# Attention of a two-layer decoder trunk: two units under way, scores and maxima of the next unit ahead of the current one's transposes

## The chip, the cores and the metric

The kernel runs on one core of one Trainium2 chip. The metric is device time in microseconds (us). Within the core, TensorE (PE) multiplies matrices into PSUM, VectorE (DVE) does elementwise work and reductions, ScalarE (ACT) does exponentials, copies and casts, GpSimd (POOL) does elementwise work in SBUF, and SyncE (SP) issues DMAs. Each engine works through its own list of instructions in order and waits on the others by semaphores.

## The reference, cut to what matters

A layer of gated DeltaNet comes first and is not touched. The second layer is sparse attention with three branches over 256 tokens. The change lies in its branches, its gate projection and its output projection:

```
q = rope(proj[..., :1024])                 # 16 heads of 64, 4 key groups
z = proj[..., 1024:4096]                   # one gate of 64 for each head and branch
sc = einsum(q, k_cmp) * scale;  p_cmp = masked_softmax(sc, ...);  o_cmp = p_cmp @ v_cmp
ss = einsum(q, ks) * scale;     p_sel = masked_softmax(ss, ...);  o_sel = p_sel @ vs
sw = einsum(q, kw) * scale;     p_win = masked_softmax(sw, ...);  o_win = p_win @ vw
o = sum over branches of sigmoid(gates) * o_branch * silu(z)
y = o @ w_out;  x = layer_norm(alpha * x + y)
```

With 256 tokens all four selection blocks are chosen, so that a query sees 256 keys in the selection branch, 256 in the window branch and 16 compressed ones.

## The kernel before, in words

The 256 tokens are two tiles of 128, t = 0 and t = 1. Attention is cut into 24 **units**: a unit of the first tile holds two heads (their later keys are masked, so that 128 keys each remain), a unit of the second tile holds one head with all 256 keys. The string `UNITS` says in which order the units of the two tiles follow each other. A unit (t, h) goes through these steps, whose names are those of tiles in the traces:

- `scores`: four PE matmuls into `s` (PSUM, two buffers, L1318).
- `maxima`: DVE adds the masks in `s` and reduces the maxima `mx` (L1331 to L1334 for a unit of the second tile, L1327 to L1329 for the first).
- `exps`: ACT's exponentials `pt` and `Pc` (L1351, L1352; L1347, L1348).
- `transposes`: four PE transposes into `ptp` (L1360), and one of `Pc` (L1362) where a pair of heads is complete. `ptp` lies in the PSUM bank `t`, of which there is one.
- `probs`: ACT copies `ptp` to SBUF as `PT` (L1367), and `PcT` (L1371).
- `readout`: PE multiplies with the values into `op` (L1386, L1389, L1392). `op` lies in the PSUM bank `o`, of which there is one. A unit of the second tile writes half of a bank, the odd head of a pair the other half. When the pair is complete `total`, five DVE operations (L1400 to L1404), scales and sums `op` into `zz`; it is deferred and put down at the next `step()`.

Three sorts of work stand among these steps. `fill(n)` takes n pieces from a list and puts them on PE. First these are pieces of the gate projection `pbz` (six matmuls of 512 columns, L233 to L235), then of the output projection: `pbo` for the first tile and `pbl` for the second (twelve of 256 columns). A piece calls for its weight, whose rounding is an ACT cast (`hi_`, L181) and whose remainder is a POOL subtraction (`lo_`, L185). Four pieces end a bank of `pbz`; ACT's `th` and DVE's `zz` (L1218, L1219) follow. `presplit()` puts down one cast ahead. A **merge** (`merge`, L1413) transposes finished columns of the output on PE into `tp_b` (L1418), which is in the same single bank `t` as `ptp`; ACT (`x1h`, L1422) and then DVE (`x1l`, L1423) read it out. Merges make the pieces of the output projection possible.

Nothing reorders these: each engine has them as the loop over the units (L1477 to L1508) writes them down. `FA[i]` and `FB[i]` are the numbers of pieces in the two places of iteration i. Before the change one unit is begun and transposed in the same iteration, and the unit before it is read out between:

```
scores(i)  [maxima(i) for a first-tile unit before the merges]  probs(i-1)  maxima(i)
fill(FA[i])  merge  presplit  exps(i)  readout(i-1)  fill(FB[i])  transposes(i)
```

The last projection pieces come after the loop.

Of the kernel before, what the change touches and what calls it, by code (L numbers as in the profile page):

```python
# [34 lines left out]

FIRST = (1, 2)

UNITS = "001010101101101101111111"
FA = "3113111011210212044211123"
FB = "0211121311122110212111000"  # L40

PRE, TAIL = 4, 2
NEG = -1e30
# [50 lines left out]
def trunk(ctx: ExitStack, tc: tile.TileContext, I: dict, out: bass.AP):  # L94
# [9 lines left out]
    def defer(n, f):  # L104
        late.append([n, f])

    def step():
        for e in late:
            e[0] -= 1
        due = [e for e in late if e[0] <= 0]  # L110
        late[:] = [e for e in late if e[0] > 0]
        for _, f in due:
            f()
# [82 lines left out]
    def lower():  # L196
        while lows:
            lows.pop(0)()
# [42 lines left out]
    def presplit():  # L241
        oldest = next(i for i, n in enumerate(uses) if n)
        split_to(min(state["top"] + PRE, oldest + NSPL, state["s"] + 1))
        lower()

    def fill(n, low=True):
        for _ in range(n):
            step()
            if fills:
                fills.pop(0)()  # L250
            if low:
                lower()
# [25 lines left out]
    first = ring.tile([P, 1024], F32, tag="raw", name="raw_first", bufs=NRAW)  # L278
# [731 lines left out]
    def sbank(name):  # L1010
        return ps_.tile([P, 2, 512], F32, tag="s", name=name)
# [4 lines left out]
    def obank(name):  # L1016
        return pt_.tile([P, 512], F32, tag="o", name=name)
# [203 lines left out]
    def zview(t, c0, n):  # L1221
        i, o = c0 // 1536, c0 % 1536
        return zz[2 * t + i][:, o:o + n]

    def need_z(t, cols):
        while not all((c, t) in zdone for c in range(-(-cols // 512))):
            fill(1)
# [76 lines left out]
    order1 = [(1, h) for h in range(16)]  # L1304
    units = [order0.pop(0) if k == "0" else order1.pop(0) for k in UNITS]
    S_, PT_, PTT, PC, PCT, MX, TP = {}, {}, {}, {}, {}, {}, {}
    cnt = {"n": 0}

    def scores(u):
        t, h = u  # L1310
        sp = S_[u] = sbank(f"s{t}{h}")
        for j in range(2):
            hh = h + j if t == 0 else h
            lq = qT[hh // 8][:, hh % 8, t * P:(t + 1) * P]
            n = 272 if t == 0 or j == 0 else 256
            c0 = 272 if t == 1 and j == 1 else 0
            for i, kk in enumerate((kh, kl)):
                PE.matmul(sp[:, j, 0:n], lq, kk[:, hh // 4, c0:c0 + n], start=i == 0, stop=i == 1)  # L1318

    def maxima(u):  # L1320
        t, h = u
        sp = S_[u]
        cm = cb[:, C_CM0:C_CM0 + 272] if t == 0 else cb[:, C_CM1:C_CM1 + 272]
        mx = MX[u] = sm.tile([P, 6], F32, tag="mx", name=f"mx{t}{h}", bufs=4)
        s4 = sp[:, :, 0:256].rearrange("p j (b k) -> p j b k", b=2)
        if t == 0:
            V.tensor_tensor(sp[:, :, 0:272], sp[:, :, 0:272], cm[:, None, :].to_broadcast([P, 2, 272]), op=ALU.add)  # L1327
            V.tensor_reduce(mx[:, 0:4].rearrange("p (j b) -> p j b", j=2), s4, axis=AX.X, op=ALU.max, negate=True)
            V.tensor_reduce(mx[:, 4:6], sp[:, :, 256:272], axis=AX.X, op=ALU.max, negate=True)  # L1329
        else:  # L1330
            V.tensor_tensor(sp[:, 1, 0:256], sp[:, 1, 0:256], cm[:, 0:256], op=ALU.add)  # L1331
            V.tensor_tensor(sp[:, 0, 256:272], sp[:, 0, 256:272], cm[:, 256:272], op=ALU.add)
            V.tensor_reduce(mx[:, 0:2], s4.rearrange("p j b k -> p b j k"), axis=AX.XY, op=ALU.max, negate=True)
            V.tensor_reduce(mx[:, 4:5], sp[:, 0, 256:272], axis=AX.X, op=ALU.max, negate=True)  # L1334

    def exps(u):
        t, h = u
        sp, mx = S_[u], MX[u]
        s4 = sp[:, :, 0:256].rearrange("p j (b k) -> p j b k", b=2)
        pt = PT_[u] = wk.tile([P, 2, 2, P], F32, tag="hl", name=f"pt{t}{h}", bufs=3)  # L1340
        if t == 0 or h % 2 == 0:
            PC[t, h] = wk.tile([P, 2, 16], F32, tag="Pc", name=f"Pc{t}{h}", bufs=4)
        Pc = PC[t, h - h % 2]
        if t == 0:
            for j in range(2):
                for b in range(2):
                    S.activation(pt[:, j, b, :], s4[:, j, b, :], AF.Exp, bias=mx[:, 2 * j + b:2 * j + b + 1])  # L1347
                S.activation(Pc[:, j, :], sp[:, j, 256:272], AF.Exp, bias=mx[:, 4 + j:5 + j])  # L1348
        else:
            for b in range(2):  # L1350
                S.activation(pt[:, :, b, :], s4[:, :, b, :], AF.Exp, bias=mx[:, b:b + 1])  # L1351
            S.activation(Pc[:, h % 2, :], sp[:, 0, 256:272], AF.Exp, bias=mx[:, 4:5])  # L1352
# [22 lines left out]
    def readout(t, h, half=None):  # L1375

        g_ = h // 4
        if half != 1:
            need_z(t, (h + 2) * 192)
            OP[t] = obank(f"op{t}{h}")  # L1380
        o3 = OP[t][:, 0:390].rearrange("p (r b d) -> p r b d", r=2, b=3)
        for r in range(2) if half is None else (half,):
            PT = PTT[0, h] if t == 0 else PTT[1, h + r]
            for b in range(2):
                if t == 0:
                    PE.matmul(o3[:, r, 1 + b, :], PT[:, r, b, :], vt_[:, b, 0, g_, :], start=True, stop=True)  # L1386
                else:
                    for j in range(2):
                        PE.matmul(o3[:, r, 1 + b, :], PT[:, j, b, :], vt_[:, b, j, g_, :], start=j == 0, stop=j == 1)  # L1389
        if half == 0:  # L1390
            return
        PE.matmul(o3[:, :, 0, :], PCT[t, h], vbd[:, g_, :, :], start=True, stop=True)  # L1392
        rc = sm.tile([P, 2, 3], F32, tag="rc", name=f"rc{t}{h}")
        o4 = o3[:, :, :, 0:64]

        o_ = zview(t, h * 192, 128).rearrange("p (r d) -> p r d", r=2)

        def total():

            V.reciprocal(o3[:, :, :, 64], o3[:, :, :, 64])  # L1400
            V.tensor_tensor(rc, o3[:, :, :, 64], gt[:, t, h * 3:h * 3 + 6].rearrange("p (r b) -> p r b", b=3), op=ALU.mult)
            V.tensor_tensor(o4, o4, zview(t, h * 192, 384).rearrange("p (r b d) -> p r b d", r=2, b=3), op=ALU.mult)
            V.tensor_tensor(o4, o4, rc[:, :, :, None].to_broadcast([P, 2, 3, 64]), op=ALU.mult)
            V.tensor_reduce(o_, o4.rearrange("p r b d -> p r d b"), axis=AX.X, op=ALU.add)  # L1404
            summed.add((t, h))

        defer(1, total)
# [45 lines left out]
    def add_bo(t, pairs):  # L1453
        for c, part in pairs:
            fills.append(lambda c=c, part=part: bo_unit(t, c, part))

    merges, ready = [], []
    cnt["t0"] = 0

    def advance():  # L1460
        if merges:
            merges.pop(0)()

    def merge0(q):
        merge(0, 4 * q, 4, tbank)
        if q:
            add_bo(0, [(c, part) for c in range(2) for part in range(4)])

    def merge1(g_):
        need_z(1, 3072)  # L1470
        merge(1, 2 * g_, 2, tbank)
        add_bo(1, [(0, g_)])
        if g_ == 3:
            add_bo(1, [(1, g_)])

    n = len(units)
    for i in range(n + 1):  # L1477
        if i < n:
            scores(units[i])
        first = i < n and units[i][0] == 0 and not merges  # L1480
        if first:

            maxima(units[i])
        if i:
            probs(units[i - 1])
        step()
        if i < n and not first:
            maxima(units[i])
        fill(int(FA[i]))
        advance()  # L1490
        presplit()
        if i < n:
            exps(units[i])
        if i:
            t, h = units[i - 1]
            if t == 0:
                readout(t, h)
                if h == 14:
                    cnt["t0"] = 1
                    merges += [lambda: merge0(0), lambda: merge0(1)] + ready  # L1500
            else:

                if (units[i - 2] if h % 2 else units[i]) == (1, h ^ 1):
                    readout(t, h - h % 2, h % 2)
                elif h % 2:
                    readout(t, h - 1)
                if h % 4 == 3:
                    (merges if cnt["t0"] else ready).append(lambda g_=h // 4: merge1(g_))  # L1508
        fill(int(FB[i]))
        if i < n:  # L1510
            transposes(units[i])
    while len(merges) > 1:
# [78 lines left out]
```

## Time and profile before

| what | value |
|---|---|
| median of 3 runs | 393.89 us (393.65 to 393.94) |
| the profiled execution: its own time | 393.75 us |
| its span, first to last instruction | 391.9 us |
| PE busy | 379.6 us, 97% of the span |
| DVE, ACT, POOL busy | 223.6, 220.6, 246.3 us |
| mean granted clock of TensorE | 0.994 |

The profiled execution took 393.75 us, of which 391.9 are the span and some 1.85 lie around it. A row of a timeline gives the start in us from the span's beginning, the duration, the engine, the line, the operation with output and input, the number of instructions merged into the row and, in brackets, the idle time ahead of it with what ended it. Matmuls are pipelined: a row's duration is longer than the distance from its start to the next start, so that PE's pace is read from starts.

### The profile page before, as it was taken

The page shows a single profiled execution, that of the slowest core. Times are in us where ns is not written, and L with a number is a line of the kernel's source. Part 1 is how long each engine was busy: PE and PEld are TensorE (multiplying, and loading weights), DVE is VectorE, ACT ScalarE, POOL GpSimd, SP SyncE. Part 2 cuts the span into 40 slices and gives each one's busy share as a digit, 9 for nine tenths or more (in the row PEclk, how much of TensorE's full clock was granted, in tenths as well). Part 3 has the DMA queues.
Part 4 walks back from the last instruction along what each step waited for, and adds up shares of the span by engine and source line. Part 5 has one row for each costly group of instructions (what it writes and reads, how often), then busy time and mean ns, then how long its engine had stood idle before and what let it go on. Part 6 is the DMA issues. An engine that isn't in the chain of part 4 may idle for free.

```text
span 391.9 us, 7551 instructions
## 1 busy us (share of the span) xinstructions
PE 379.6 (97%) x2870; PEld 335.5 (86%) x2870; DVE 223.6 (57%) x591; ACT 220.6 (56%) x433; POOL 246.3 (63%) x154
## 2 busy tenths in 40 slices
PE   8999999999999999999999999999999999999991
PEld 6999999999989987877998788888888888878891
DVE  2868776668623445463641755545656465676726
ACT  4688666656663462625563649566474747456410
POOL 5699999747444846894764988193544637209051
PEclk9999999999999999999999999999999999999997
DMA  7876578654334315573736764243415243301011
GB/s 226 324 223 221 206 232 291 190 135 164 110 110 138 125 35 186 163 248 125 204 118 214 278 223 150 103 153 115 164 39 175 64 153 109 107 3 54 3 54 54
DMA packets 23476, 58.68 MB, mean 150 GB/s; under 512 B 6672, under 2 KB 9232, under 8 KB 23312
## 3 DMA queue, kind: packets, MB, share of 16 engines
q1 hardware_dynamic: 23232, 58.13, 44.9%
q8 instruction: 22, 0.36, 0.4%
q14 instruction: 14, 0.11, 0.1%
q10 hardware_dynamic: 144, 0.07, 0.1%
q0 software_dynamic: 64, 0.01, 0.0%
HBM read 55.96 MB, written 2.23 MB: 148 GB/s over the span
## 4 chain that ended last, share of the span: by engine, by line
PE 42%; DVE 4%; ACT 3%; DMA 2%; POOL 2%; issue 1%; POOLq 0%; DVEq 0%; SPq 0%; ACTq 0%
PE pbz L233 6%; PE pbz L234 6%; PE pbz L235 6%; PE op L1389 4%; PE s L1318 3%; PE ptp L1360 3%; PE op L1392 2%; PE op L1386 1%; DMA raw_bz<-in_bz 1%; ACT hi_bq L181 1%; POOL lo_bq L185 1%; PE pskv L235 1%; PE pbo L233 1%; PE pskv L233 1%; PE pskv L234 1%; PE qtp L1205 1%
## 5 line engine op out<-in xcount | busy, mean ns | idle before, releaser
L185 POOL TENSOR_TENSOR lo_bz<-raw_bz,hi_bz 128x1024 fp32r<-128x1024 f32 x24 | 56.8, 2387 | 39.3 <-ACT hi_bz L181 21.7
L185 POOL TENSOR_TENSOR lo_wqkv<-raw_wqkv,hi_wqkv 128x1024 fp32r<-128x1024 f32 x22 | 52.6, 2408 | 6.7 <-ACT hi_wqkv L181 4.5
L233 PE MATMUL pbz<-hi_bz,x1h 128*128 128x512 f32 x96 | 38.9, 405 | 0.0
L234 PE MATMUL pbz<-hi_bz,x1l 128*128 128x512 f32 x96 | 37.7, 393 | 0.0
L235 PE MATMUL pbz<-lo_bz,x1h 128*128 128x512 f32 x96 | 37.6, 392 | 0.0
L185 POOL TENSOR_TENSOR lo_bo<-raw_bo,hi_bo 128x1024 fp32r<-128x1024 f32 x8 | 18.9, 2390 | 22.8 <-ACT hi_bo L181 17.7
L185 POOL TENSOR_TENSOR lo_skv<-raw_skv,hi_skv 128x1024 fp32r<-128x1024 f32 x12 | 28.4, 2399 | 5.0 <-PE pskv L235 5.0
L185 POOL TENSOR_TENSOR lo_wz<-raw_wz,hi_wz 128x1024 fp32r<-128x1024 f32 x8 | 19.4, 2440 | 16.9 <-ACT hi_wz L181 16.8
L1367 ACT COPY PT<-ptp 128x512 f32<-128x512 f32 x24 | 14.1, 588 | 24.0 <-PE ptp L1360 24.0
L181 ACT CAST hi_bz<-raw_bz 128x1024 fp32r<-128x1024 f32 x24 | 25.2, 1052 | 2.9 <-DMA raw_bz<-in_bz 1.6
L185 POOL TENSOR_TENSOR lo_wo<-raw_wo,hi_wo 128x1024 fp32r<-128x1024 f32 x8 | 18.9, 2385 | 11.5 <-ACT hi_wo L181 11.5
L185 POOL TENSOR_TENSOR lo_bq<-raw_bq,hi_bq 128x1024 fp32r<-128x1024 f32 x8 | 19.1, 2394 | 10.8 <-ACT hi_bq L181 10.8
L181 ACT CAST hi_wqkv<-raw_wqkv 128x1024 fp32r<-128x1024 f32 x22 | 22.7, 1043 | 1.0 <-DMA raw_wqkv<-in_wqkv 1.0
L233 PEld LDWEIGHTS pbz<-hi_bz,x1h 128*128 128x128 f32 x96 | 18.0, 188 | 4.1
L235 PEld LDWEIGHTS pbz<-lo_bz,x1h 128*128 128x128 f32 x96 | 18.0, 188 | 4.1
L234 PEld LDWEIGHTS pbz<-hi_bz,x1l 128*128 128x128 f32 x96 | 18.0, 188 | 2.7
L1351 ACT ACTIVATE pt<-s,mx 128x256 f32<-128x256 f32 x32 | 13.4, 472 | 11.0 <-DVE mx L1334 8.8
L215 PE MATMUL pk<-xh,hi_wqkv 128*128 128x256 f32 x64 | 18.7, 291 | 0.0
L215 PE MATMUL pq<-xh,hi_wqkv 128*128 128x256 f32 x64 | 18.5, 289 | 0.0
L217 PE MATMUL pq<-xh,lo_wqkv 128*128 128x256 f32 x64 | 18.1, 283 | 0.0
L216 PE MATMUL pk<-xl,hi_wqkv 128*128 128x256 f32 x64 | 18.1, 283 | 0.0
L217 PE MATMUL pk<-xh,lo_wqkv 128*128 128x256 f32 x64 | 18.1, 283 | 0.0
(360 smaller groups left out, 1256.1 us busy)
## 6 DMA issues: line engine op xcount, KB each, us to landing
raw_bz<-in_bz SPq DMA_DIRECT2D x24, 512.0 KB, 3.3
raw_wqkv<-in_wqkv SPq DMA_DIRECT2D x23, 512.0 KB, 4.5
raw_skv<-in_skv SPq DMA_DIRECT2D x12, 512.0 KB, 3.3
raw_wz<-in_wz SPq DMA_DIRECT2D x8, 512.0 KB, 3.4
raw_wo<-in_wo SPq DMA_DIRECT2D x8, 512.0 KB, 3.3
raw_bq<-in_bq SPq DMA_DIRECT2D x8, 512.0 KB, 3.7
raw_bo<-in_bo SPq DMA_DIRECT2D x8, 512.0 KB, 3.3
raw_w<-in_w SPq DMA_DIRECT2D x4, 512.0 KB, 3.4
```

Of the source, the lines that this page charges most:

```text
L181: S.copy(h, r)
L185: e.tensor_tensor(l, r, h.bitcast(F32), op=ALU.subtract)
L215: PE.matmul(ps[:, 0:T], wh[:, kt, :], ah[:, kt, :], start=kt == 0, stop=False)
L216: PE.matmul(ps[:, 0:T], wh[:, kt, :], al_[:, kt, :], start=False, stop=False)
L217: PE.matmul(ps[:, 0:T], wl[:, kt, :], ah[:, kt, :], start=False, stop=kt == 7)
L233: PE.matmul(ps, ah[:, kt, tt], wh[:, k4, cols], start=kt == 0, stop=False)
L234: PE.matmul(ps, al_[:, kt, tt], wh[:, k4, cols], start=False, stop=False)
L235: PE.matmul(ps, ah[:, kt, tt], wl[:, k4, cols], start=False, stop=kt == 7)
L1318: PE.matmul(sp[:, j, 0:n], lq, kk[:, hh // 4, c0:c0 + n], start=i == 0, stop=i == 1)
L1351: S.activation(pt[:, :, b, :], s4[:, :, b, :], AF.Exp, bias=mx[:, b:b + 1])
L1367: S.copy(PT.rearrange("p a b c -> p (a b c)"), TP[u])
L1389: PE.matmul(o3[:, r, 1 + b, :], PT[:, j, b, :], vt_[:, b, j, g_, :], start=j == 0, stop=j == 1)
```

## The change

Each iteration now begins the next unit. Its scores and maxima stand behind the readout of the unit before, its exponentials at the end, ahead of the current unit's transposes:

```
probs(i-1)  fill(FA[i])  presplit  readout(i-1)
scores(i+1)  maxima(i+1)  merge  fill(FB[i])  exps(i+1)  transposes(i)
```

The first unit is begun ahead of the loop. `UNITS` puts the eight first-tile units at the places 0, 1, 4, 5, 7, 9, 10 and 11 of 24 (before: 0, 1, 3, 5, 7, 10, 13 and 16). `FA` is 2 up to iteration 13 and 1 from there on; `FB` is 1 up to iteration 12, then 0 1 0 1 0 1 and then 0. Readouts are grouped by the rule of before.

```
-UNITS = "001010101101101101111111"
+UNITS = "001100101000111111111111"
...
     n = len(units)
+
+    def begin(u):
+        scores(u)
+        maxima(u)
+
+    begin(units[0])
+    fill(1)
+    exps(units[0])
     for i in range(n + 1):
-        if i < n:
-            scores(units[i])
-        first = i < n and units[i][0] == 0 and not merges
-        if first:
-
-            maxima(units[i])
         if i:
             probs(units[i - 1])
         step()
-        if i < n and not first:
-            maxima(units[i])
-        fill(int(FA[i]))
-        advance()
+        merge_ = merges.pop(0) if merges else None
+        fill(int(FA[i]) - (i == 0))
         presplit()
-        if i < n:
-            exps(units[i])
         if i:
...
+        if i + 1 < n:
+            begin(units[i + 1])
+        if merge_:
+            merge_()
         fill(int(FB[i]))
+        if i + 1 < n:
+            exps(units[i + 1])
         if i < n:
             transposes(units[i])
```

What this moves is shown at three places. In the names `s114` is the score bank of tile 1, head 14; the other names go the same way, and the number behind the underscore is the tile's own.

First PE, around the merge `tp_b12` of the second tile. Before:

```order
L1318 MATMUL s113_4275<-kl_2283,qT1_2691 128x256
L233 MATMUL pbo00_4198<-hi_bo_3_4005,x1h_2043 128x512
...
L1418 MATMUL tp_b12_4297<-ident_112,zz2_3270 128x128 x2
L1389 MATMUL op112_4306<-vtok_2284,PT112_4280 128x65 x4
L233 MATMUL pbo10_4314<-hi_bo_4_4199,x1h_2043 128x512
...
L1360 MATMUL ptp113_4321<-ident_112,pt113_4302 128x128 x4
```

And in the change:

```order
L1389 MATMUL op18_4187<-vtok_2284,PT18_4175 128x65 x4
L1318 MATMUL s110_4192<-kh_2282,qT1_2691 128x272
L1318 MATMUL s110_4192<-kl_2283,qT1_2691 128x272
L1318 MATMUL s110_4192<-kh_2282,qT1_2691 128x256
L1318 MATMUL s110_4192<-kl_2283,qT1_2691 128x256
L1418 MATMUL tp_b12_4202<-ident_112,zz2_3275 128x128 x2
L1360 MATMUL ptp19_4212<-ident_112,pt19_4166 128x128 x4
L1362 MATMUL s19_4141<-ident_112,Pc18_4111 32x128
```

Before, a readout and a piece of six matmuls stood between the merge's transposes and the next use of the bank `t`; now `ptp19` follows at once.

Second PE at the end of the units. Before:

```order
L1389 MATMUL op114_4405<-vtok_2284,PT114_4377 128x65 x4
L1360 MATMUL ptp115_4410<-ident_112,pt115_4401 128x128 x4
L1362 MATMUL s115_4372<-ident_112,Pc114_4357 32x128
...
L1389 MATMUL op114_4405<-vtok_2284,PT115_4416 128x65 x4
L1392 MATMUL op114_4405<-vbd_2386,PcT114_4418 128x2x65
```

And in the change:

```order
L1318 MATMUL s115_4433<-kl_2283,qT1_2691 128x256
L1360 MATMUL ptp114_4447<-ident_112,pt114_4400 128x128 x4
L1389 MATMUL op114_4459<-vtok_2284,PT114_4452 128x65 x4
L1360 MATMUL ptp115_4464<-ident_112,pt115_4443 128x128 x4
L1362 MATMUL s115_4433<-ident_112,Pc114_4401 32x128
L1389 MATMUL op114_4459<-vtok_2284,PT115_4470 128x65 x4
L1392 MATMUL op114_4459<-vbd_2386,PcT114_4472 128x2x65
```

Before, 36 matmuls of `pbl` stood where the dots are, and 12 of `pbo` between `s115` and `op114`; now no projection stands between `s115` and the end of the readouts.

Third DVE and ACT in the last units. DVE's row around the sum of `op112` in the change (before, the five operations on `op112` stood ahead of the four on `s115`):

```order
L1331 TENSOR_TENSOR s115_4433<-s115_4433,cb_2278 128x256
L1332 TENSOR_TENSOR s115_4433<-s115_4433,cb_2278 128x16
L1333 TENSOR_REDUCE mx115_4438<-s115_4433 128x2
L1334 TENSOR_REDUCE mx115_4438<-s115_4433 128x1
L1400 RECIPROCAL op112_4380<-op112_4380 128x6
L1401 TENSOR_TENSOR rc112_4432<-op112_4380,gt_2972 128x6
L1402 TENSOR_TENSOR op112_4380<-op112_4380,zz3_3805 128x6x64
L1403 TENSOR_TENSOR op112_4380<-op112_4380,rc112_4432 128x6x64
L1404 TENSOR_REDUCE zz3_3805<-op112_4380 128x128
```

And ACT's row around the exponentials of unit 113 in the change:

```order
L1351 ACTIVATE pt113_4348<-s113_4338,mx113_4343 128x2x128 x2
L1352 ACTIVATE Pc112_4292<-s113_4338,mx113_4343 128x16
L1367 COPY PT112_4357<-ptp112_4352 128x512
L945 ACTIVATE x1_2042<-x1_2042,nb_blw0_4312,mv_blw0_4308 128x512
L1422 CAST x1h_2043<-tp_b14_4395 128x2x128
```

The copy `PT` of a unit now stands behind the exponentials of the unit after it (before, it stood ahead of them), and the sum of a finished pair behind the maxima of a unit begun later.

## Rows read from the trace of the kernel before

**Rows 1.** All that PE waited for from 250 us on: total, times, longest.

```profile
PE op L1389 <- DVE zz L1404: 0.6, 2, 0.4
PE tp_b L1418 <- ACT PT L1367: 0.2, 1, 0.2
```

**Rows 2.** PE's timeline through one iteration without a wait.

```profile
351.30 0.60 PE L1360 MATMUL ptp<-ident,pt 128*128 128x128 f32 x4
...
351.76 0.37 PE L1318 MATMUL s<-kh,qT 128*128 128x272 f32 x1
...
352.33 0.39 PE L233 MATMUL pbo<-hi_bo,x1h 128*128 128x512 f32 x1
...
353.72 0.38 PE L1418 MATMUL tp_b<-ident,zz 128*128 128x128 f32 x2
353.94 1.00 PE L1389 MATMUL op<-vtok,PT 128*128 128x65 f32 x8
...
355.29 0.50 PE L233 MATMUL pbo<-hi_bo,x1h 128*128 128x512 f32 x1
...
356.79 0.60 PE L1360 MATMUL ptp<-ident,pt 128*128 128x128 f32 x4
357.14 0.37 PE L1318 MATMUL s<-kh,qT 128*128 128x272 f32 x1
```

**Rows 3.** PE's timeline around the first tile's two merges.

```profile
342.95 0.28 PE L1318 MATMUL s<-kl,qT 128*128 128x256 f32 x1
343.37 0.66 PE L1418 MATMUL tp_b<-ident,zz 128*128 128x128 f32 x4
344.21 2.00 PE L1389 MATMUL op<-vtok,PT 128*128 128x65 f32 x16 [0.19 <-DVE zz L1404]
...
347.42 0.28 PE L1318 MATMUL s<-kl,qT 128*128 128x256 f32 x1
347.89 0.65 PE L1418 MATMUL tp_b<-ident,zz 128*128 128x128 f32 x4 [0.19 <-ACT PT L1367]
348.91 1.11 PE L1389 MATMUL op<-vtok,PT 128*128 128x65 f32 x8 [0.37 <-DVE zz L1404]
```

**Rows 4.** DVE's timeline: maxima, a pair's sum, a merge's remainder, a gate.

```profile
341.34 0.69 DVE L1219 SCALAR_TENSOR_TENSOR zz<-th,pbz 128x512 f32<-128x512 f32 x1 [0.49 <-ACT th L1218]
...
345.36 0.17 DVE L1334 TENSOR_REDUCE mx<-s 128x1 f32<-128x16 f32 x1
345.44 0.68 DVE L1423 TENSOR_TENSOR x1l<-tp_b,x1h 128x512 fp32r<-128x512 f32 x1
...
352.54 0.43 DVE L1331 TENSOR_TENSOR s<-s,cb 128x256 f32<-128x256 f32 x1 [1.71 <-PE s L1318]
...
353.83 0.16 DVE L1334 TENSOR_REDUCE mx<-s 128x1 f32<-128x16 f32 x1
354.55 0.43 DVE L1423 TENSOR_TENSOR x1l<-tp_b,x1h 128x256 fp32r<-128x256 f32 x1 [0.55 <-ACT x1h L1422]
...
365.67 0.20 DVE L1400 RECIPROCAL op<-op 128x6 f32<-128x6 f32 x1 [0.42 <-PE op L1392]
...
367.31 0.56 DVE L1404 TENSOR_REDUCE zz<-op 128x128 f32<-128x384 f32 x1
```

**Rows 5.** ACT's timeline: exponentials and copies of second-tile units.

```profile
345.62 0.84 ACT L1351 ACTIVATE pt<-s,mx 128x256 f32<-128x256 f32 x2 [0.97 <-DVE mx L1334]
...
347.25 0.59 ACT L1367 COPY PT<-ptp 128x512 f32<-128x512 f32 x1 [0.63 <-PE ptp L1360]
...
350.32 0.84 ACT L1351 ACTIVATE pt<-s,mx 128x256 f32<-128x256 f32 x2 [1.15 <-DVE mx L1334]
...
351.20 1.05 ACT L181 CAST hi_bo<-raw_bo 128x1024 fp32r<-128x1024 f32 x1
```

**Rows 6.** Stretches at the end: length, busy of PE, PEld, DVE, ACT, POOL; PEclk, DMA.

```profile
384.00:385.00 1.00, 0.05 (x1) 0.00 (x0) 0.97 (x3) 0.00 (x0) 0.00 (x0) 1.00 0.00 0
...
386.00:387.00 1.00, 0.00 (x0) 0.00 (x0) 0.91 (x2) 0.00 (x0) 0.92 (x2) 0.94 0.00 0
```

More of the change, by code (lines that the diff above doesn't have):

```diff
@@ L36 @@
 FIRST = (1, 2)
-UNITS = "001010101101101101111111"
-FA = "3113111011210212044211123"
-FB = "0211121311122110212111000"
+UNITS = "001100101000111111111111"
+FA = "2222222222222211111111111"
+FB = "1111111111111010101000000"
 PRE, TAIL = 4, 2
@@ L1497, in trunk @@
                 readout(t, h)
[L1498 to L1508, printed above, removed]
+            elif (units[i - 2] if h % 2 else units[i] if i < n else 0) == (1, h ^ 1):
+                readout(t, h - h % 2, h % 2)
+            elif h % 2:
+                readout(t, h - 1)
+            if (t, h) == (0, 14):
+                cnt["t0"] = 1
+                merges += [lambda: merge0(0), lambda: merge0(1)] + ready
+            if t and h % 4 == 3:
+                (merges if cnt["t0"] else ready).append(lambda g_=h // 4: merge1(g_))
+        if i + 1 < n:
+            begin(units[i + 1])
+        if merge_:
+            merge_()
         fill(int(FB[i]))
+        if i + 1 < n:
+            exps(units[i + 1])
         if i < n:
```

## The prediction, as it was made

> **What bounds the kernel now.** I read the waits first. From the start of the attention on, PE waited three times, 0.8 us in all [rows 1]. PE's timeline shows the same: one block starts where the last leaves off, with a piece of projection between any two steps of a unit [rows 2]. So PE's list of work is the bound, and the change leaves that list as it is in content: the same matmuls in another order. The time can only move by what PE waits, and by what a change of operand type costs. Around the first tile's merges PE loses more than the page's waits say [rows 3]: 0.42 and 0.47 us from the last score matmul to the merge, where the spacing of 0.23 us for 512 columns (1.39 us for six, [rows 2]) gives 0.12 for 256, and 0.84 and 1.02 us for four merge transposes, where two take 0.22 [rows 2]. That is 0.30 + 0.35 + 0.40 + 0.58 = 1.63 us. The readouts behind those waits last 0.11 us more than plain ones (1.11 against 1.00, [rows 2, 3]), twice: 1.85 us. This is all that a better order could take away.
>
> **PE's cover.** I price each block by its distance to the next [rows 2]: a piece behind scores 1.39 us, a piece behind float32 work (transposes, a readout) 1.50, `ptp` 0.35, with `Pc` 0.46, a merge of two transposes 0.22, of four 0.44. A piece of `pbl`, twelve matmuls of half the columns, is taken as a piece of six, 1.50.
>
> **The chains that must fit under it.** Let T be the end of the scores that an iteration begins. DVE starts on them 0.21 us later (352.33 to 352.54, [rows 2, 4]). The four operations run 1.29 us to the start of the last, and DVE can start something else 0.08 behind that (345.36 to 345.44): T + 1.58. The maxima themselves are there 0.09 later, T + 1.67. ACT starts the exponentials 0.09 after the maxima (345.53 to 345.62, [rows 4, 5]) and is free 0.88 later (350.32 to 351.20). Three things now stand behind these on their engines:
> - ACT's copy `PT` of the unit before: 1.67 + 0.09 + 0.88 + 0.59 + 0.05 until PE goes on (347.84 to 347.89, [rows 3, 5]) = **T + 3.27**. The next readout waits for it.
> - DVE's sum of a finished pair: 2.20 us (365.67 to 367.87, [rows 4]); 1.58 + 2.20 + 0.05 = **T + 3.83**. The next readout that opens the bank `o` waits for it; the bank is single, and the row of before shows exactly this wait [rows 1].
> - DVE's `x1l` of a merge, 0.43 us, or 0.68 for a merge of four: **T + 2.06 or T + 2.31**. The next `ptp` waits for it, since `ptp` and `tp_b` share the bank `t`. The trace of before has no such wait, because a readout and a piece stand between; its bounds are nothing and these two numbers, and I take these, since the order of the change puts `x1l` behind the four operations on the scores and `ptp` directly behind `tp_b`.
>
> **Iterations 0 to 12.** Behind the scores stand a piece, `ptp` and two pieces: 1.39 + 0.35 + 1.50 + 1.39 = 4.63 us. The longest chain is the sum with a gate's `zz` ahead of it (0.62 us from start to start of a following operation, taken as 0.69 less the 0.08 overlap): 4.45 us. It is covered, by 0.2 us; the copy by 1.3 us. So no gain there, since there was no wait before [rows 1], and no loss.
>
> **Iterations 13 to 23,** with one piece ahead of the readout and mostly none behind the scores. PE's waits, one after the other:
> - 13: merge of four, then `ptp` at once: 2.31 - 0.44 = 1.87.
> - 14: merge of four and a piece, 1.94, `ptp` waits 0.37 and goes on at 2.31; behind 0.35 + 1.50 the readout would start at 4.16, but DVE has maxima, `x1l`, a gate and a sum, 1.58 + 0.60 + 0.62 + 2.20 + 0.05 = 5.05: 0.89 more. 1.26.
> - 15, 17, 21: merge of two, then `ptp`: 2.06 - 0.22 = 1.84 each, 5.52. The piece behind `ptp` then covers the copy.
> - 16, 18: a piece, `ptp`, a piece, 3.24, against the sum's 3.83: 0.59 each, 1.18.
> - 19: `ptp` with `Pc` and a piece, 1.96, against the copy's 3.27: 1.31.
> - 20: `ptp` and a piece, 1.85, against the sum's 3.83: 1.98.
> - 22: `ptp` alone, 0.35, against the sum's 3.83: 3.48.
> - 23: the last `ptp` runs 0.60 us, then 0.59 for the copy and some 0.1 for two handovers, 1.29 - 0.46 = 0.83 before the last readout.
>
> Together 17.43 us. Each iteration then lasts 5 to 6.5 us, longer than DVE's 1.58 + 0.43 + 2.20 in it, so that DVE is free at each T, as assumed. Of the twelve waits seven are ahead of a readout, which then lasts 0.11 more: 0.8. Those ahead of `ptp` I cost at nothing more (bound 0.1 each).
>
> **Changes of type.** The first piece behind float32 work costs 1.50 - 1.39 = 0.11 us more than one behind scores [rows 2]. Such a change from float32 to the rounded type occurs 39 times in the attention before and 46 times in the change's order, because scores stand alone between a readout and `ptp` in the late iterations: 7 x 0.11 = 0.8 us.
>
> **What moves for nothing.** The maxima a unit ahead and the exponentials ahead of `ptp` take `ptp`'s own wait away; there was hardly one to take. The first-tile units moved up bring the merges five iterations earlier; the output projection then runs between the last units, where it covers, and is missing behind them: the 36 matmuls of `pbl` ahead of the last readout are gone from there, which is what 22 and 23 pay. From the last readout on, PE's list is the same in both, and so is the layer norm's tail. Casts and remainders are as many as before and are called for a unit earlier or later; their cover is the weights that are kept ahead, and if it were gone a piece would wait for at most a cast and a remainder.
>
> **The sum:** 393.75 + 17.43 + 0.8 + 0.8 - 1.85 = 410.9 us, 4.3% above. The profiled execution is 0.14 us under the median of the runs, so I say **411.0**.
>
> **The rivals.**
> - *TensorE's clock falls in the longest wait.* At the end of the trace the last matmul ends at 384.05, the granted clock is full from 384 to 385, and its mean is 0.94 from 386 to 387 [rows 6]: with nothing to do it went to the lower level, half, within 3 us. The wait of iteration 22, 3.5 us, is as long. What follows on PE is some 10 us of matmuls; at half speed to the end that is up to 10 us more, for a part of them 2 to 3 us: 413 to 414, at most 421. Against it: the readout and `ptp` stand on either side, and no wait inside the trace of before was long enough to show it. The Trainium skill's page "TensorE: Matmul & The Clock Gate", section "Why this matters for your kernels", warns of this: idle gaps between bursts of matmuls take the clock to its lower level, and only steady work brings it back. By that rule this change is one to avoid, and the sum would be about 413.
> - *The early iterations do not fit either.* Their margin is 0.2 us where a gate stands ahead of a sum. A first-tile unit's maxima and exponentials are longer than those of the second tile, and a cast ahead of the exponentials takes 1.05 us [rows 5]. At 0.4 us in each of twelve, 4.8: 416.
> - *The late waits are smaller.* If the handovers between engines overlap and each of the twelve waits is 0.3 to 0.5 shorter, 407 to 405.
> - *Faster: two units under way hide everything.* It is one mechanism: PE has at each readout 3.83 us of other work behind the scores. Then the 1.85 us of before fall away and the changes of type cost 0.8: 392.7. It holds in iterations 0 to 12; it decides where the late covers reach 3.83, and only iteration 14 comes to that by its work. For it: the exponentials, the longest step, are off `ptp`'s path. Against: the copy and the sum were moved behind another unit's work on the same engines.
> - *The change does not do what it says:* the rows of the order show the scores and maxima ahead, so I give it nothing.
>
> **How the numbers follow.** The forecast 57%, the clock 20%, the early iterations 9%, smaller late waits 10%, everything hidden 4%. The forecast's own range is 408 to 413 (0.2 us either way for each wait). From 405 to 416 the range takes in the smaller waits, the lesser part of the clock and most of the early iterations. About 0.2%, 0.8 us, is what a measurement of this kernel can tell from no change. The last case alone lies under that: faster 0.03, within 0.02, slower 0.95.
>
> **What would show it.** Right: PE's waits list `ptp` behind DVE `x1l` four or five times with about 1.8 us, `op` behind DVE `zz` L1404 with up to 3.5 us, and `op` behind ACT `PT` with about 1 us, nearly all in the last 60 us of the attention, and hardly one before. Wrong: the waits lie in the first half; or PE is still without gaps at the end; or the granted clock is half in the last 10 us of PE's work, which is the first rival.

## The result, and the profile after

The changed kernel takes **427.46 us** (424.51 to 429.15, 6 runs), the kernel before 393.91 in the same comparison: a ratio of **1.0836 [1.0811, 1.0862]**. Slower, as forecast, but by 33.6 us where 17.1 were forecast, and outside the range.

The profiled execution spans 426.0 us, against 391.9. I read first how long TensorE worked and how long it stood, from its first score matmul to its last matmul: the same 864 records in both kernels. The columns of this view are length, PE's busy time (and its rows), granted clock, DMA share and GB/s. Before:

```profile
240.90:384.10 143.20, 142.27 (x864) 1.00 0.28 95
```

After:

```profile
240.67:418.10 177.43, 157.16 (x864) 0.91 0.22 77
```

The stretch is 34.2 us longer, and it falls into two parts. PE stands for 177.43 - 157.16 = 20.3 us, where it stood for 0.9: 19.3 more. And the same matmuls keep it busy for 14.9 us more: the granted clock was 0.91 of full in the mean, so for about 2 x 0.09 x 177 = 32 us it was at the lower of its two levels, 1.2 in place of 2.4 GHz. The forecast had most of the first part; in its sum the second is nothing.

The waits of PE after (total, times, longest), to be held against [rows 1]:

```profile
PE op L1389 <- DVE zz L1404: 7.2, 5, 3.4
PE ptp L1360 <- DVE x1l L1423: 7.0, 5, 1.7
PE s L1318 <- DVE gt L1297: 3.7, 1, 3.7
...
PE pbl L233 <- DVE x L905: 1.0, 1, 1.0
...
PE pbz L235 <- POOL lo_bz L185: 0.8, 1, 0.8
...
PE op L1389 <- ACT PT L1367: 0.5, 1, 0.5
```

Two of these are the forecast's two great waits. The third, 3.7 us on the scores, is not in the forecast. PE's timeline of after has these waits with their places, all but the 0.8 us for `lo_bz`; the number in brackets is the idle time ahead of the row:

```profile
247.83 0.57 PE L1318 MATMUL s<-kh,qT 128*128 128x272 f32 x1 [3.67 <-DVE gt L1297]
...
343.07 0.66 PE L1360 MATMUL ptp<-ident,pt 128*128 128x128 f32 x4 [1.71 <-DVE x1l L1423]
...
349.37 0.66 PE L1360 MATMUL ptp<-ident,pt 128*128 128x128 f32 x4 [0.38 <-DVE x1l L1423]
...
352.16 1.08 PE L1389 MATMUL op<-vtok,PT 128*128 128x65 f32 x8 [0.74 <-DVE zz L1404]
...
355.66 1.12 PE L1360 MATMUL ptp<-ident,pt 128*128 128x128 f32 x4 [1.66 <-DVE x1l L1423]
...
365.01 1.08 PE L1389 MATMUL op<-vtok,PT 128*128 128x65 f32 x8 [0.58 <-DVE zz L1404]
...
368.58 0.73 PE L1360 MATMUL ptp<-ident,pt 128*128 128x128 f32 x4 [1.73 <-DVE x1l L1423]
...
378.06 1.08 PE L1389 MATMUL op<-vtok,PT 128*128 128x65 f32 x8 [0.59 <-DVE zz L1404]
...
381.88 0.39 PE L233 MATMUL pbl<-hi_bo,x1h 128*128 128x256 f32 x1 [0.95 <-DVE x L905]
...
388.90 1.38 PE L1389 MATMUL op<-vtok,PT 128*128 128x65 f32 x8 [1.95 <-DVE zz L1404]
...
393.22 1.12 PE L1360 MATMUL ptp<-ident,pt 128*128 128x128 f32 x4 [1.52 <-DVE x1l L1423]
...
402.55 1.38 PE L1389 MATMUL op<-vtok,PT 128*128 128x65 f32 x8 [3.36 <-DVE zz L1404]
...
405.46 0.90 PE L1389 MATMUL op<-vtok,PT 128*128 128x65 f32 x3 [0.46 <-ACT PT L1367]
```

The last twelve stand in the iterations from 13 on, 15.6 us in all. The clock, by stretches (columns as above):

```profile
244.00:260.00 16.00, 12.33 (x56) 0.79 0.19 66
260.00:340.00 80.00, 79.08 (x434) 1.00 0.37 125
340.00:355.00 15.00, 11.17 (x71) 1.00 0.20 71
355.00:360.00 5.00, 4.34 (x19) 0.66 0.00 1
```

```profile
370.00:375.00 5.00, 5.00 (x23) 0.76 0.00 0
...
390.00:395.00 5.00, 3.48 (x17) 0.50 0.14 52
...
405.00:410.00 5.00, 4.54 (x20) 0.50 0.00 0
```

It is full for the eighty microseconds in which PE hardly waits, and falls once around the first long wait and four times among the late ones.

### The profile page after: what moved, and what is told of

It is laid out like the page before. It is cut to its first block, busy times and chain, and to the rows that moved or that the text cites. A ratio compares the mean times of both kernels' runs of the same rounds, so it can differ in the third digit from the quotient of the medians.

```text
span 426.0 us, 7547 instructions
## 1 busy us (share of the span) xinstructions
PE 394.1 (93%) x2870; PEld 345.5 (81%) x2870; DVE 221.5 (52%) x591; ACT 218.7 (51%) x433; POOL 246.2 (58%) x154
## 5 line engine op out<-in xcount | busy, mean ns | idle before, releaser
L233 PE MATMUL pbz<-hi_bz,x1h 128*128 128x512 f32 x96 | 39.8, 415 | 0.0
L1331 DVE TENSOR_TENSOR s<-s,cb 128x256 f32<-128x256 f32 x16 | 6.9, 432 | 49.2 <-PE s L1318 49.2
L913 POOL TENSOR_SCALAR mv_blw<-mv_blw 128x1 f32<-128x1 f32 x2 | 1.0, 500 | 47.5 <-DVE mv_blw L912 47.5
L1389 PEld LDWEIGHTS op<-vtok,PT 128*128 128x128 f32 x128 | 17.6, 209 | 10.8 <-ACT PT L1367 8.8
L1389 PE MATMUL op<-vtok,PT 128*128 128x65 f32 x128 | 18.3, 292 | 7.7 <-DVE zz L1404 7.2
L1360 PE MATMUL ptp<-ident,pt 128*128 128x128 f32 x96 | 16.6, 300 | 7.0 <-DVE x1l L1423 7.0
L1347 ACT ACTIVATE pt<-s,mx 128x128 f32<-128x128 f32 x32 | 10.1, 372 | 23.8 <-DVE mx L1329 18.2
L1360 PEld LDWEIGHTS ptp<-ident,pt 128*128 128x128 f32 x96 | 12.8, 155 | 10.7 <-DVE x1l L1423 8.5
```

The costliest lines, as they stand in the source:

```text
L233: PE.matmul(ps, ah[:, kt, tt], wh[:, k4, cols], start=kt == 0, stop=False)
L1360: PE.transpose(tp[:, (2 * j + b) * P:(2 * j + b + 1) * P], pt[:, j, b, :], ident)
```

## The experiments

**1. The gates at once.** ACT's and DVE's rows of after show where the 3.67 us come from:

```profile
243.11 1.28 ACT L1347 ACT_TABLE_LOAD   x1 [1.02 <-DVE mx L1329]
244.41 0.62 ACT L1347 ACTIVATE pt<-s,mx 128x128 f32<-128x128 f32 x2
...
245.74 0.28 ACT L1292 ACTIVATE gq<-gq 128x96 f32<-128x96 f32 x1
```

```profile
246.05 0.27 DVE L1293 TENSOR_SCALAR gq<-gq 128x96 f32<-128x96 f32 x1 [3.04 <-ACT gq L1292]
...
247.44 0.24 DVE L1297 TENSOR_SCALAR gt<-gq,cb 128x16 f32<-128x16 f32 x1
```

The attention's gates lie in `gq`, which is one of the two score buffers. They are read out two steps later (`defer(2, gates)`), on ACT behind the first unit's exponentials and the table load of 1.28 us ahead of these, and then by four operations of DVE. With one unit under way the second buffer was not needed before that. With two, iteration 0 begins the second unit's scores, which need it at once.

```
-    defer(2, gates)
+    gates()
```

> The gates of the attention (an exponential and four VectorE operations that read a score bank) are computed at once instead of two steps later; nothing else differs from the change. Theory (the second unit's scores, now begun in the first iteration, wait 3.7 us for the bank that the gates still read, and TensorE's clock falls in that wait): the wait of 3.7 us goes and with it the half-speed stretch behind it, some 2.7 us; 421 us, and the granted clock is full up to the late iterations. Rival (the wait at the start is not the gates', or the time is lost elsewhere): 427 us as the change.

Measured 423.94 us, 1.0757 [1.0698, 1.0815]: 3.5 us less than the change by the medians, 3.1 by the ratios, whose intervals leave 2.5 us either way, and between the two expectations. The wait for `gt` is gone, but another has come:

```profile
252.23 1.11 PE L1386 MATMUL op<-vtok,PT 128*128 128x65 f32 x8 [1.63 <-ACT PT L1367]
...
254.86 0.63 PE L233 MATMUL pbz<-hi_bz,x1h 128*128 128x512 f32 x1
```

The copy now stands behind the second unit's exponentials, and the first 512-column matmul behind this wait lasts 0.63 us, where one at the full clock lasts 0.39 [rows 2]: the clock has fallen here too, which the theory did not expect. So the bank costs some 3 us net, and the first iterations have less cover than the forecast gave them.

**2 and 3. The tables alone, the loop alone.** One kernel has the old loop with the new `UNITS`, `FA` and `FB`; the other the new loop with the old tables.

```
 # 2: loop as before                     # 3: loop as after
+UNITS = "001100101000111111111111"      +UNITS = "001010101101101101111111"
+FA = "2222222222222211111111111"        +FA = "3113111011210212044211123"
+FB = "1111111111111010101000000"        +FB = "0211121311122110212111000"
```

> The loop of before with the three tables of the change (order of units, pieces of projection per place). Theory (the loop's order causes the waits, the tables little): waits only around the last two units, about 5 us, no wait at the start; 398 to 401 us. Rival (spreading the projection over the last units and moving the first-tile units up is what costs): most of the loss stays, above 412 us.

> The loop of the change with the three tables of before. Theory (the loop's order causes the waits): the copy behind the next unit's exponentials, the sum behind the next maxima and the merge ahead of the transposes make about 17 us of waits here too, spread over more of the attention since pieces are laid out for the other loop, and the clock falls in the longest of them; 411 to 420 us. Rival (the tables cost it): under 400 us.

Measured 403.55 us, 1.0239 [1.0197, 1.0281], for the tables, above the 398 to 401 of the theory, and 420.21, 1.0644 [1.06, 1.0689], for the loop, at the upper end of its theory. Against a loss of 33.6 us for both, the loop alone brings 26, the tables alone 9. With the tables alone PE's waits are few, 4.1 us in all, the largest group is for the exponentials, and none is for a merge:

```profile
PE ptp L1360 <- ACT pt L1351: 2.3, 4, 0.7
```

These waits do not make the 9 us by themselves. The stretch from the first score matmul to the last matmul, and in it the one around the longest wait (1.31 us up to 378.06, for a pair's sum):

```profile
241.00:393.90 152.90, 148.52 (x864) 0.97 0.27 89
...
377.00:390.00 13.00, 11.46 (x55) 0.61 0.00 0
```

PE stands 3.5 us longer than before and is busy 6.2 us longer for the same matmuls, with the clock at its lower level for most of the 13 us. So some two thirds of what the tables cost is the clock, and a single wait of 1.3 us stands at its fall.

With the loop alone those of after are back, the one for the bank among them:

```profile
PE op L1389 <- DVE zz L1404: 5.8, 5, 3.2
PE ptp L1360 <- DVE x1l L1423: 3.7, 4, 1.7
...
PE s L1318 <- DVE gt L1297: 2.3, 1, 2.3
```

**4. TensorE kept at work in its waits.** The changed kernel with matmuls put into the waits. Their weights are zero and they go to the projection bank that is open, so that they add nothing to it. The order of all other work stays.

```
+    def idle(k):
+        for _ in range(k):
+            PE.matmul(state["open"][:, 0:256], zer, warm, start=False, stop=False)
+    AT_PTP = {13: 13, 14: 2, 15: 13, 17: 13, 21: 12}
+    AT_OP = {15: 6, 17: 4, 20: 8, 21: 16, 23: 28, 24: 4}
...
         presplit()
+        idle(AT_OP.get(i, 0))
...
+        if i == 0:
+            idle(30)
         if i + 1 < n:
             begin(units[i + 1])
...
         if i < n:
+            idle(AT_PTP.get(i, 0))
             transposes(units[i])
```

> The change, with matmuls of a zero weight put into PE's waits: they add zero to a projection bank that is open anyway, 30 ahead of the second unit's scores, 12 to 13 between the merges and the transposes, 4 to 28 ahead of readouts that wait. Every wait is still there, but PE works in it. Theory (the clock falls because PE idles in those waits, and that costs some 13 us beyond the waits): mean clock 0.985 or more, 412 to 417 us. Rival (the clock falls for another reason, or the waits alone make the time): clock and time as the change, 427 us, or longer.

Measured 417.58 us, 1.0584 [1.0547, 1.0622], just above the theory's range, with the mean clock at 0.993. More work, and 9.9 us less time than the change (the intervals leave 1.8 either way), at one and the same order of everything else. The late iterations ran at the full clock:

```profile
340.00:360.00 20.00, 19.31 (x129) 1.00 0.14 49
...
380.00:408.20 28.20, 27.25 (x221) 1.00 0.06 20
```

So the clock is worth the 9.9 us at least. It is more, since the 149 added matmuls have a price: twelve of them start within 1.50 - 0.27 us of each other,

```profile
245.26 1.50 PE L1486 MATMUL pbz<-const-bfloat16-1.0,zer 128*128 128x256 bf16 x12
```

0.112 us each, 16.7 us in all, where the waits that they fill were 15.4 (20.3 less the 4.9 that this kernel still stands). The upper bound is what PE's busy time grew by, less the 0.8 of the forecast's type changes: 14.1. The clock costs 10 to 14 us.

**5 to 7. The order on VectorE and ScalarE mended.** Three kernels from the changed one: the merge ahead of the readout (5); the copy ahead of the next exponentials and the pair's sum ahead of the next maxima (6); both and the gates at once (7). The edit of 5, and then that of 6:

```
         merge_ = merges.pop(0) if merges else None
         fill(int(FA[i]) - (i == 0))
+        if merge_:
+            merge_()
         presplit()
...
             begin(units[i + 1])
-        if merge_:
-            merge_()
```

```
             probs(units[i - 1])
+        if 0 < i < n:
+            exps(units[i])
         step()
...
                 (merges if cnt["t0"] else ready).append(lambda g_=h // 4: merge1(g_))
+        step()
         if i + 1 < n:
             begin(units[i + 1])
...
         fill(int(FB[i]))
-        if i + 1 < n:
-            exps(units[i + 1])
```

> The changed kernel with one thing moved: a merge begins right behind the first group of projection pieces, ahead of the pair's readout, instead of behind the next unit's maxima. Theory A (the chains stand one behind another on VectorE, and only the one that ends last is paid): TensorE's seven waits for x1l, 7.0 us in the changed kernel's trace, go, but the readout and the maxima behind the merge move back by its 1.2 to 1.5 us, so the copy of the transposed exponentials, 3.3 us behind the scores with about 2 us of matmuls to cover it, becomes the late one in iterations 13, 15, 17 and 21 with about 1.3 us each: 2 to 4 us gained, 423 to 425 us. Theory B (each wait is a loss of its own): all 7.0 us go, and with the clock that falls in them 3 to 5 us more, 415 to 417 us. No effect: 427 us.

> The changed kernel with the order on ACT and DVE put back in two places: the copy of the transposed exponentials ahead of the next unit's exponentials, and the sum of a pair's totals ahead of the next unit's maxima. Theory A: the waits for the row scale, 7.2 us in five, fall to about 1.5 to 2 us (only the one of 3.4 us leaves a part of itself), the merges' waits grow by at most 2 us because the maxima start later, so 2 to 6 us are gained by waits and up to 4 us by the clock: 417 to 425 us. Theory B (the exponentials then come later than the transposes that read them need): new waits of the transposes on ACT as long as those removed, 427 us or more.

> The changed kernel with four orders changed at once: the gates at once instead of two steps later, the merge ahead of the readout, the copy ahead of the next exponentials, the sum ahead of the next maxima; the table of units, the spread of the projection and the two units under way stay. Theory A (the loss is the order in which ACT and DVE reach what TensorE needs, and the clock that falls in those waits): 3.7, 7.0 and some 5 us of the waits go and most of 10 us of the clock with them, 398 to 403 us. Theory B (two units under way cost what they cost in whatever order, since the cover between the scores of an iteration and its readout is too short): the waits change their names and keep their sum of some 20 us, 415 to 424 us. Faster than the kernel before (under 393.1 us) would show that the loop's depth is worth something by itself.

Measured: (5) 421.37 us, 1.0685 [1.0656, 1.0714]; (6) 419.38, 1.0628 [1.0599, 1.0657]; (7) 406.34, 1.0302 [1.0266, 1.0339]. The waits of 5:

```profile
PE op L1389 <- DVE zz L1404: 4.6, 3, 3.4
...
PE op L1389 <- ACT PT L1367: 3.4, 4, 1.2
PE tp_b L1418 <- ACT PT L1367: 2.3, 2, 1.4
```

The 7.0 us for `x1l` are gone, and the copy's waits are 5.7 us where they were 0.5: four ahead of the readout, of which two of 1.2 us stand in iterations 15 and 17 as theory A had it, and two ahead of the merge's own transposes, which it had not. The gain of 6 us is above A's 2 to 4 and below B's 10: zz's waits shrank as well, by 2.6. The waits of 6:

```profile
PE ptp L1360 <- DVE x1l L1423: 8.6, 5, 1.8
...
PE op L1389 <- DVE zz L1404: 1.3, 1, 1.3
```

The sum's waits fall from 7.2 to 1.3, the merges' grow by 1.6; 8 us gained, within A. In 7 the three large groups of after shrink at once, while those for `lo_bz` grow from 0.8 to 1.9,

```profile
PE ptp L1360 <- DVE x1l L1423: 2.5, 2, 1.5
PE pbz L235 <- POOL lo_bz L185: 1.9, 3, 0.8
PE op L1389 <- DVE zz L1404: 1.3, 1, 1.3
```

and the time is 3 us above A's upper end but far from B's 415: the order made most of the loss. But mended, the loop is still slower than before: over the same 864 matmuls PE stands 6.2 us longer and is busy 5.3 longer.

**8. Pieces held back for the first tile's merges.** The kernel before, its tables alone changed, so that a piece of projection stands ahead of each of the two merges.

```
-FA = "3113111011210212044211123"
-FB = "0211121311122110212111000"
+FA = "3113111011210211011111123"
+FB = "0211121311111110200111000"
```

> The kernel before with one change in its two tables of projection pieces: some pieces are held back until the units that the first tile's merges stand in, where TensorE waited 1.85 us in all in its trace. Theory A: these waits are covered and nothing else changes, 1.6 to 1.85 us less, a ratio of 0.9953 to 0.996 (392.0 to 392.3 us beside 393.9). Theory B: the pieces were the cover of waits that are just hidden where they stood, and the waits return there: 393.5 to 395 us.

Measured 392.24 us, 0.9951 [0.9931, 0.9972], in 12 runs: 1.9 us less (1.1 to 2.7), theory A. PE's busy time in the stretch is now its length but for 0.03 us:

```profile
241.24:382.55 141.31, 141.28 (x864) 1.00 0.30 96
```

This is the fastest of all kernels here. The 1.85 us around the merges [rows 3] could be taken away, and with 0.03 us of standing left there is no further wait in this stretch for an order to hide.

**9. Both missing terms taken out.** Kernel 4 with the gates at once and thirteen such matmuls in iteration 1 in place of the thirty in iteration 0.

```
-    defer(2, gates)
+    gates()
...
+        if i == 1:
+            fill(1)
+            idle(13)
+        fill(int(FA[i]) - (i < 2))
...
-        if i == 0:
-            idle(30)
```

> The changed kernel with both things that the forecast lacked taken out: the gates at once, and matmuls with weights of zero in TensorE's waits (they add nothing to the bank that they go to), so that its clock doesn't fall. Theory A (the two add up with the waits that the forecast had): the wait of 3.7 us for the score bank becomes one of 1.6 us for the copy, as in the kernel with the gates alone, and the clock stays up, so about 2 us less than the kernel with such matmuls alone: 415 to 416 us, which is 393.9 plus 15.6 of late waits, 1.6 early, 0.8 for the projection's low parts, 0.8 for more changes of type, less 1.85, or 411 us, plus some 4 us that no term covers yet. Theory B (nothing is left over, and the 4 us go with the gates): 411 to 412 us.

Measured 415.28 us, 1.0541 [1.0499, 1.0583], as theory A had it. Its stretch:

```profile
240.56:404.85 164.29, 159.61 (x996) 1.00 0.25 83
```

Against before, 3.8 us more of standing and 17.3 more of work, of which the 132 added matmuls at 0.112 are 14.8. Of the 2.5 left 0.8 can be the forecast's type changes; I put the rest to the changes between these bf16 matmuls and the others, which no run measured apart. If that holds, some 2 of the 4 us that stood uncovered are the price of the experiment, and the kernel without that price would take about 413.

**10. The mended loop with the old tables.** Kernel 7 with the tables of before.

```
+UNITS = "001010101101101101111111"
+FA = "3113111011210212044211123"
+FB = "0211121311122110212111000"
```

> The new loop, two units under way, with the four orders mended (the gates at once, the merge ahead of the readout, the copy ahead of the next exponentials, the sum ahead of the next maxima) and with the three tables of the kernel before. Theory A (the tables cost what they cost in the old loop, 403.6 us, and the mended loop costs next to nothing): 394 to 397 us, and no gain since TensorE is the bound either way. Theory B (the loop's depth has a price of its own in any order): 400 to 406 us. Under 393.1 us: the depth is worth something with pieces of the projection to cover it.

Measured 399.69 us, 1.0133 [1.009, 1.0176]: between the two, 0.3 us below B's lower end and 2.7 above A's upper one. Around the first tile's merges stand three waits of half a microsecond and more, and behind the third the clock is half:

```profile
346.86 0.66 PE L1418 MATMUL tp_b<-ident,zz 128*128 128x128 f32 x4 [0.57 <-ACT PT L1367]
...
351.01 0.66 PE L1360 MATMUL ptp<-ident,pt 128*128 128x128 f32 x4 [0.56 <-DVE x1l L1423]
...
352.34 1.12 PE L1418 MATMUL tp_b<-ident,zz 128*128 128x128 f32 x4 [0.68 <-ACT PT L1367]
```

```profile
352.00:355.00 3.00, 2.66 (x13) 0.53 0.00 0
```

Over the whole stretch PE stands 2.5 us longer than before and is busy 4.1 longer:

```profile
241.82:391.60 149.78, 146.40 (x864) 0.98 0.27 91
```

In a table, medians in us (the mended loop has the gates at once too):

| loop | tables before | tables after |
|---|---|---|
| before | 393.9 | 403.6 |
| after | 420.2 | 427.5 |
| after, mended | 399.7 | 406.3 |

Two units under way brought no gain in either column. With the old tables PE had next to no wait that they could hide; with the new ones the loop of before has 4.4 us of standing, and the mended loop stands 7.1. No run has tables fitted to the mended loop, pieces held ahead of its merges as in experiment 8 for instance, so that its best time stays open.

## Why the prediction was wrong, and where it was right

**Right: the bound, and the late waits.** Measured against the forecast, iteration by iteration: 13, 1.71 for 1.87; 14, 0.38 + 0.74 for 0.37 + 0.89; 15, 17 and 21, 1.66, 1.73 and 1.52 for 1.84 each; 16 and 18, 0.58 and 0.59 for 0.59; 20, 1.95 for 1.98; 22, 3.36 for 3.48; 23, 0.46 for 0.83. Only 19 has another cause: 0.95 in the middle of the piece of `pbl`, for a bank that `pbo` had filled and that DVE reads out at L905, behind the four operations on the scores (381.15 to 381.83), where the copy was forecast with 1.31 behind the piece. Together 15.63 against 17.43. The chains T + 2.06, T + 3.27 and T + 3.83 are confirmed by experiments 5 and 6 too: move one link and the next chain comes forward, at its own price.

**The step that failed first: "Iterations 0 to 12".** It ended "and no loss", and it looked only at chains on DVE and ACT that begin at T. Iterations 1 to 12 bear it out: from 260 to 340 us PE stood for 0.9 us, 0.78 of it a late `lo_bz`. But iteration 0 begins two units at once, and the second's bank was not free: 3.67 us. A chain that ends in the release of a projection's or a score bank was not in the list; the 0.95 us of iteration 19 are a second one. Experiment 1 takes the first away, net some 3 us.

**The step that failed worst: the clock as a rival with 20%, priced at "2 to 3 us", at most 10, and only for the wait of iteration 22.** It fell around the first wait and then four times among late waits of 0.4 to 3.4 us; the last of these is the one that the rival named, behind iteration 22. It cost 10 to 14 us (experiment 4 and the busy time), more than any single term but the late waits. "No wait inside the trace of before was long enough to show it" was taken as evidence against; it was no evidence, as the trace of before has only three waits, of 0.19 to 0.37 us. The sum with both: 411.0 as forecast, less 1.8 for the late waits, plus 3.7 for the bank, 0.8 for `lo_bz` and 10 to 14 for the clock, is 424 to 428; 427.46 was measured.

The Trainium skill bears on this in two places of its page "TensorE: Matmul & The Clock Gate". The section that the prediction cited, "Why this matters for your kernels", warns of long idle gaps between bursts of matmuls; the trace agrees that idleness lowers the clock, but three of the five falls here came behind waits of only 1.66 to 1.95 us. The section "A second HAM failure mode: psum-queue depth-cycling" speaks of short idle times between groups of matmuls, frequent enough that the clock swings between its levels. The trace agrees, with five falls in one execution. It gives no price, but it would have sent the forecast to every late wait and not to the longest alone.

**The small terms.** The 1.85 us around the merges are confirmed (experiment 8, 1.9 with 1.1 to 2.7). Restarts and type changes, 0.8 each, lie within what experiment 4 can't separate from its own cost; they stay estimates.

**The rival on the other side, everything hidden,** falls with experiments 7 and 10: even with the order mended no kernel with two units under way came below before, on either set of tables.

## What to carry to other kernels

Where the bounding engine has hardly a wait, a deeper pipeline has hardly anything to gain, and each of the kernels with it here had more waits than before: look first for the waits that it would hide, and cover those (here 1.85 us, which two strings of digits gained). When a unit is begun earlier, list every buffer it writes with the last reader of its former content, the first iteration included, and not only the chains on the engines. And when a change lets the bounding engine wait often, price the clock for the stretch in which the waits crowd: here each microsecond of waiting cost another half to three quarters (10 to 14 us on 19). That is no fixed rate: with the tables alone 6.2 us of added busy time came with 3.5 us of added waiting.

## What the runs showed of the hardware

- The clock did not follow the length of the last wait. In the change a wait of 1.71 us up to 343 us left it full until 355; in one of 1.66 up to 355.66 it fell, and the next five microseconds have 0.66 in the mean. With the mended loop and old tables three waits of 0.57, 0.56 and 0.68 within 6 us went ahead of a fall (0.53 from 352 to 355), and in the kernel with the gates alone one of 1.63 did. In kernel 6 four waits for `x1l`, of 1.66 to 1.79 us, between 343 and 369 us left it full from 340 to 380.
- The same kernel's executions differ with it: the change's six times go from 424.51 us at a mean granted clock of 0.969 to 429.15 at 0.954.
- Matmuls with zero weights in the waits kept the clock up and paid for themselves: 149 of them, 0.112 us each, shortened the execution by 9.9 us.
